# Column sums of the late modulation vectors: from four 32-column products and a second pass to eight products with one moving column

## The chip, the core and the metric

The kernel runs on one NeuronCore of a Trainium2 chip. The metric is device time in microseconds (us) of one execution. The engines are TensorE (PE, its weight loads PEld), VectorE (DVE), ScalarE (ACT), GpSimd (POOL) and SyncE (SP), which issues nearly all DMAs. Each engine takes its instructions in the order in which they stand in its queue.

## What is computed

One layer of a decoder: a gated DeltaNet mixer and a SwiGLU channel mixer, each followed by a residual and a layer norm, with six modulation vectors worked out from a conditioning vector `c`. For one sequence of 256 tokens and a model width of 2048:

```
cond = jax.nn.silu(c)
mod = (cond @ mod_w[i] + mod_b[i])[:, None, :]
sh1, sc1, ga1, sh2, sc2, ga2 = jnp.split(mod, 6, axis=-1)
h = x * (1 + sc1) + sh1
y = gated_deltanet(h, ...)
x = layer_norm(ALPHA_DN * x + (1 + ga1) * y, ln_g[i, 0], ln_b[i, 0])
h = x * (1 + sc2) + sh2
y = swiglu(h, ffn_w_gu[i], ffn_w_down[i])
x = layer_norm(ALPHA_DN * x + (1 + ga2) * y, ln_g[i, 1], ln_b[i, 1])
```

The change touches how `ga1`, `sc2`, `sh2` and `ga2` are worked out. Each has 2048 numbers and is kept as a tile of 128 partitions by 16 columns, so that number 128·j + p stands in partition p of column j.

## The kernel before

**The projections.** All large products are in f32 precision, split in two parts. A weight block of 128 x 1024 is loaded into `raw` (L188), ACT rounds it to `wh` (L197), and DVE subtracts to get the rest `wl` (L198). TensorE then makes three products of 512 columns for each k tile and each of the two token tiles (L233 to L235). A `Group` runs these over its k tiles in chunks of four. The groups go over `w_in`, then `w_out`, then `ffn_w_gu`, then `ffn_w_down`. Between them, the DeltaNet steps (convolution, the solves, the state) run as tasks.

**The late modulation vectors.** `mods_late` works out one vector of 2048 in two halves of 1024 columns. For each half, 16 blocks `mraw` of 128 x 1024 from `mod_w` are loaded by SP (L342, two buffers). DVE multiplies each by one number a partition, from `cond`, and adds it into `macc` (one buffer; L281 for the first, L282 for the other 15). After the sixteenth, `macc` holds 128 partial sums a column, and TensorE has to add them up over the partitions. The half is closed in these steps:
- four products (L361), each with a column of ones, widened to 32 columns, as weights and 256 columns of `macc` as the moving operand; product j goes to the 32 PSUM partitions from 32·j on;
- `to_columns`: ACT copies the 128 x 256 sums from PSUM to SBUF (`sums`, L287), and two products (L290) with 128 columns of `sums` as weights and four columns of the identity as the moving operand turn them into columns, in a second PSUM tile;
- DVE adds `mod_b` and, for three of the vectors, one, and writes eight columns of the vector (L365).

`ga1`, `sc2` and `sh2` are worked out during the `w_in` and `w_out` groups, `ga2` during the `ffn_w_gu` groups: 8 halves. `to_columns` is also called four times at the start, for `sc1` and `sh1`; these calls stay. The PSUM tiles of both steps come from the tag `tp`, of two buffers, which the transposes use too; `sums` shares the tag `hf`, of two buffers.

**What sets the order.** The code gives each piece of work a priority, a due time counted in projection steps (`at`, `spawn`, `advance`). A scheduler deals the instructions out to the engines' queues by these priorities and by its own estimate of when operands are ready. So a change of the instructions in one place can shift others in the queues. The groups over `ffn_w_gu`, but for the first, keep TensorE's instructions in the order in which they are written.

Of the kernel before, what the change touches and what calls it, by code (L numbers as in the profile page):

```python
# [12 lines left out]
OP = mybir.AluOpType  # L13
# [16 lines left out]
def gdn_layer_kernel(ctx: ExitStack, tc: tile.TileContext, x, c, mod_w, mod_b, ln_g, ln_b,  # L30
# [21 lines left out]
    stt = nc.vector.scalar_tensor_tensor  # L52
    mm = nc.tensor.matmul
# [36 lines left out]
    def tp():  # L90
        return psum.tile([128, 512], F32, name="tp", tag="tp", bufs=2)
# [26 lines left out]
    ones = upper[:, 127:128]  # L118
# [14 lines left out]
    p = tp()  # L133
# [16 lines left out]
    p = tp()  # L150
    tr(p[:, :96], brow[:96], ident[:96, :96])
    modb = consts.tile([128, 96], F32, name="modb")
# [126 lines left out]
    def mac(acc, w, k):  # L279
        if k == 0:  # L280
            return ts(acc, w, cond[:, 0:1], None, op0=OP.mult)  # L281
        return stt(acc, w, cond[:, k:k + 1], acc, op0=OP.mult, op1=OP.add)  # L282

    def to_columns(p, hw, nb):

        acc = work.tile([128, 256], F32, name="sums", tag="hf", bufs=2)
        act(acc[:, 0:hw], p[:, 0:hw], AF.Copy)  # L287
        q = tp()
        for i in range(nb):
            mm(q[:, 4 * i:4 * i + 4], acc[:, i * 128:(i + 1) * 128], ident[:, 0:128:32], start=True, stop=True)  # L290
        return q[:, 0:4 * nb].rearrange("p (i j) -> p j i", j=4)
# [44 lines left out]
    def mods_late(dst, j0, plus, every, pin=False):  # L336

        def load(i):
            raw = stream.tile([128, 1024], F32, name="mraw", tag="mraw", bufs=2)
            half, k = divmod(i, KT)  # L340
            c0 = j0 * 128 + half * 1024
            nc.sync.dma_start(raw, mod_w2[k * 128:(k + 1) * 128, c0:c0 + 1024])  # L342
            return raw

        ahead = [load(0)]
        for i in range(2 * KT):
            half, k = divmod(i, KT)
            if i + 1 < 2 * KT:
                ahead.append(load(i + 1))
            if k == 0:  # L350
                acc = work.tile([128, 1024], F32, name="macc", tag="macc", bufs=1)
            yield every / 2
            ins = mac(acc, ahead.pop(0), k)
            if pin and i == 0:
                tc.keep_in_program_order(ins)
            yield every / 2
            if k == KT - 1:
                yield MACW
                p = tp()
                for j in range(4):  # L360
                    mm(p[32 * j:32 * j + 32, 0:256], ones.to_broadcast([128, 32]), acc[:, j * 256:(j + 1) * 256],  # L361
                       start=True, stop=True)
                qv = to_columns(p, 256, 2)
                j = half * 8
                stt(dst[:, j:j + 8].rearrange("p (j i) -> p j i", j=4), qv, plus,  # L365
                    modb[:, j0 + j:j0 + j + 8].rearrange("p (j i) -> p j i", j=4), op0=OP.add, op1=OP.add)


    def h_tiles(tags, names):
# [549 lines left out]
    def late_mods():  # L919
        yield from mods_late(ga1, 32, 1.0, MODEVERY)  # L920
        yield from mods_late(sc2, 64, 1.0, MODEVERY)
        yield from mods_late(sh2, 48, 0.0, MODEVERY)
        tt(A2, lng[:, 0:KT], sc2, op=OP.mult)
        tt(B2, lnb[:, 0:KT], sc2, op=OP.mult)
        tt(B2, B2, sh2, op=OP.add)
# [231 lines left out]
```

## Time and profile before

| | |
|---|---|
| median of 3 runs | 2375.24 us |
| the three runs | 3448.0, 2375.24, 1709.14 us |
| the profiled execution | 1712.19 us, span 1710.4 us |
| granted TensorE clock, mean over the span | 0.994 |
| PE busy | 1656.9 us (97%) |
| DVE busy | 1138.0 us (67%) |
| ACT busy | 875.9 us (51%) |
| HBM | 229 GB/s over the span |

A row of time shows its start and its duration in us; two times in brackets say how long the engine stood idle before it and what ended that. A weight load on PEld runs ahead of the product that uses it, so several rows overlap. The starts of the weight loads show the pace of TensorE more sharply than the products' durations, whose ends are modelled.

### The profile page before, as it was taken

Reading aid. Unit: us, or ns where it says so; the run is one execution under the profiler, and the core shown is the slowest. Engines: PE = TensorE matmul, PEld = TensorE weight load, DVE = VectorE, ACT = ScalarE, POOL = GpSimd, SP = SyncE. Lnnn points to the kernel's source line nnn. Section 1 sums busy time; section 2 is a strip of 40 time slices with the busy share of each in tenths; the row PEclk is TensorE's granted clock in tenths of the full one; section 3 lists DMA queues with packets and bytes.
Section 4 is the critical chain, followed back from the end, with each engine's and each line's share of the span. In section 5 each row is a group of like instructions: output and inputs, shape, how many; then the busy total and the mean of one; then the engine's idle time right before and its main releaser. Section 6 shows DMA issues by size and latency. Waiting matters only on the chain.

```text
span 1710.4 us, 23214 instructions
## 1 busy us (share of the span) xinstructions
PE 1656.9 (97%) x8655; PEld 1322.0 (77%) x8655; DVE 1138.0 (67%) x1641; ACT 875.9 (51%) x1426; POOL 63.1 (4%) x70
## 2 busy tenths in 40 slices
PE   5999999999999999999999999999999999999996
PEld 2666787787887877888787788888888887888885
DVE  2566997958966988948776875765467544555455
ACT  2433679769568667564333644444444443433342
POOL 1000000001001000000000000000000000100002
PEclk9999999999999999999999999999999999999998
DMA  9998795535864777837888586886688666855663
GB/s 345 371 337 288 226 296 184 172 112 161 257 201 122 235 254 231 262 128 266 305 276 283 150 283 192 287 283 192 189 256 285 186 196 209 283 193 190 196 196 112
DMA packets 184434, 392.93 MB, mean 230 GB/s; under 512 B 12176, under 2 KB 14688, under 8 KB 183040
## 3 DMA queue, kind: packets, MB, share of 16 engines
q1 hardware_dynamic: 181952, 378.64, 68.1%
q0 software_dynamic: 2368, 12.80, 2.2%
q8 instruction: 68, 1.11, 0.3%
q14 instruction: 46, 0.38, 0.1%
HBM read 387.18 MB, written 4.21 MB: 229 GB/s over the span
## 4 chain that ended last, share of the span: by engine, by line
PE 73%; DVE 12%; DMA 6%; issue 4%; ACT 3%; POOL 1%; SPq 1%; POOLq 0%; DVEq 0%; ACTq 0%
PE pj L234 20%; PE pj L233 20%; PE pj L235 20%; DMA mraw<-in_mod_w_dram 6%; DVE wl L198 5%; PE gd L234 1%; PE gd L235 1%; DVE macc L282 1%; PE gd L233 1%; ACT wh L197 1%; PE tp L321 1%; DVE X L596 1%; DVE cy L480 1%; DVE tmp L594 1%; DVE LA L571 1%
## 5 line engine op out<-in xcount | busy, mean ns | idle before, releaser
L198 DVE TENSOR_TENSOR wl<-raw,wh 128x1024 fp32r<-128x1024 f32 x518 | 629.8, 1222 | 358.9 <-ACT wh L197 356.0
L197 ACT ACTIVATE wh<-raw 128x1024 fp32r<-128x1024 f32 x518 | 548.0, 1061 | 612.5 <-PE pj L235 443.3
L233 PE MATMUL pj<-wh,h2T 128*128 128x512 f32 x704 | 275.2, 391 | 0.2 <-ACT h2T L983 0.2
L235 PE MATMUL pj<-wh,h2T 128*128 128x512 f32 x704 | 274.5, 390 | 0.4 <-DVE h2T L988 0.4
L234 PE MATMUL pj<-wl,h2T 128*128 128x512 f32 x704 | 274.0, 390 | 0.0
L233 PE MATMUL pj<-wh,hT 128*128 128x512 f32 x640 | 256.5, 403 | 0.0
L234 PE MATMUL pj<-wl,hT 128*128 128x512 f32 x640 | 256.0, 400 | 0.1
L235 PE MATMUL pj<-wh,hT 128*128 128x512 f32 x640 | 255.7, 400 | 0.0
L282 DVE SCALAR_TENSOR_TENSOR macc<-mraw,cond,macc 128x1024 f32<-128x1024 f32 x120 | 153.6, 1280 | 59.1 <-DMA mraw<-in_mod_w_dram 58.5
L235 PEld LDWEIGHTS pj<-wh,h2T 128*128 128x128 f32 x704 | 132.1, 188 | 28.2 <-DVE h2T L988 0.9
L234 PEld LDWEIGHTS pj<-wl,h2T 128*128 128x128 f32 x704 | 132.2, 188 | 27.7 <-DVE wl L198 0.7
L233 PEld LDWEIGHTS pj<-wh,h2T 128*128 128x128 f32 x704 | 132.2, 188 | 27.7 <-ACT h2T L983 0.8
L233 PEld LDWEIGHTS pj<-wh,hT 128*128 128x128 f32 x640 | 120.5, 189 | 26.4 <-issue 3.3
L234 PEld LDWEIGHTS pj<-wl,hT 128*128 128x128 f32 x640 | 120.7, 189 | 24.9 <-DVE wl L198 0.9
L235 PEld LDWEIGHTS pj<-wh,hT 128*128 128x128 f32 x640 | 120.7, 189 | 23.9 <-issue 0.8
L480 DVE SCALAR_TENSOR_TENSOR cy<-tp,cw,cy 128x255 f32<-128x255 f32 (+2 forms) x192 | 85.9, 475 | 1.3 <-ACT cy L476 1.2
L234 PE MATMUL gd<-wl,hT 128*128 128x512 f32 x128 | 51.7, 406 | 1.4 <-DVE wl L198 1.4
L233 PE MATMUL gd<-wh,hT 128*128 128x512 f32 x128 | 49.8, 398 | 1.9 <-DVE part L266 1.0
L235 PE MATMUL gd<-wh,hT 128*128 128x512 f32 x128 | 51.4, 405 | 0.0
L321 PE MATMUL tp<-mraw,cond 128*32 128x256 f32 x368 | 35.4, 470 | 10.9 <-DMA mraw<-in_mod_w_dram 10.9
L234 PE MATMUL pj<-wl,oTc 128*128 128x512 f32 x112 | 43.8, 391 | 0.7 <-DVE wl L198 0.7
L233 PE MATMUL pj<-wh,oTc 128*128 128x512 f32 x112 | 43.9, 392 | 0.0
(399 smaller groups left out, 2253.6 us busy)
## 6 DMA issues: line engine op xcount, KB each, us to landing
raw<-in_gdn_w_in_dram SPq DMA_DIRECT2D x194, 512.0 KB, 4.7
mraw<-in_mod_w_dram SPq DMA_DIRECT2D x192, 512.0 KB, 5.5
raw<-in_ffn_w_gu_dram SPq DMA_DIRECT2D x176, 512.0 KB, 4.4
raw<-in_ffn_w_down_dram SPq DMA_DIRECT2D x88, 512.0 KB, 4.7
raw<-in_gdn_w_out_dram SPq DMA_DIRECT2D x64, 512.0 KB, 5.4
x<-in_x_dram SPq DMA_DIRECT2D x8, 256.0 KB, 6.2
r<-in_x_dram POOLq DMA_DIRECT2D x2, 1024.0 KB, 5.2
x1s<-r POOLq DMA_DIRECT2D x2, 1024.0 KB, 7.0
```

What stands on the lines that cost most here:

```text
L197: act(hi, raw, AF.Copy)
L198: tt(lo, raw, f32(hi), op=OP.subtract)
L233: mm(ps, sh, wh, start=start, stop=False)
L234: mm(ps, sh, wl, start=False, stop=False)
L235: mm(ps, sl, wh, start=False, stop=stop)
L282: return stt(acc, w, cond[:, k:k + 1], acc, op0=OP.mult, op1=OP.add)
L321: mm(p[32 * j:32 * j + 32, 0:hw], cond[:, k:k + 1].to_broadcast([128, 32]), raw[:, kl, j * hw:(j + 1) * hw], start=(k == 0), stop=(k == KT ...
L480: stt(y[:, o + s:o + 256], p[:, o:o + 256 - s], tap(3 - s, ct + i), y[:, o + s:o + 256], op0=OP.mult, op1=OP.add)
L571: stt(la[:, s0 + i], src, sc[:, 0, c, h:h + 1], dm[:, i, None, :].to_broadcast([128, 2, 128]), op0=OP.mult, op1=OP.mult)
L594: tt(tv, LD[:, j + 1:32, j:j + 1].to_broadcast([128, n, m]), X[:, j, None, 0:m].to_broadcast([128, n, m]), op=OP.mult)
L596: tt(X[:, j + 1:32, 0:m], X[:, j + 1:32, 0:m], tv, op=OP.subtract)
```

## The change

The closing of each half is done in one step. The 1024 columns of `macc` are eight blocks of 128 columns; each block is now the weights of a product whose moving operand is the single column of ones. The product's result is one column of 128 sums, which is already the form wanted. Eight products write eight columns of one PSUM tile, and DVE adds `mod_b` from there. The copy on ACT, the second pass and its PSUM tile are not needed in these halves any more.

```
                 yield MACW
+
                 p = tp()
-                for j in range(4):
-                    mm(p[32 * j:32 * j + 32, 0:256], ones.to_broadcast([128, 32]), acc[:, j * 256:(j + 1) * 256],
-                       start=True, stop=True)
-                qv = to_columns(p, 256, 2)
+                for i in range(8):
+                    mm(p[:, i:i + 1], acc[:, i * 128:(i + 1) * 128], ones, start=True, stop=True)
                 j = half * 8
-                stt(dst[:, j:j + 8].rearrange("p (j i) -> p j i", j=4), qv, plus,
-                    modb[:, j0 + j:j0 + j + 8].rearrange("p (j i) -> p j i", j=4), op0=OP.add, op1=OP.add)
+                stt(dst[:, j:j + 8], p[:, 0:8], plus, modb[:, j0 + j:j0 + j + 8], op0=OP.add, op1=OP.add)
```

The file gets two lines shorter, so that lines behind the change have a number lower by two: L365 becomes L364, L676 L674, L805 L803.

The queues of TensorE, at the half that closes in the first group over `w_out` (779 us in the trace; `upper` holds the column of ones, `oTa` and `oTb` are the DeltaNet's output). Before:

```order
L233 MATMUL pj<-wh,oTb 128x512
L234 MATMUL pj<-wl,oTb 128x512
L235 MATMUL pj<-wh,oTb 128x512
L361 MATMUL tp<-macc,upper 32x256 x4
L233 MATMUL pj<-wh,oTb 128x512
L234 MATMUL pj<-wl,oTb 128x512
L235 MATMUL pj<-wh,oTb 128x512
L290 MATMUL tp<-ident,sums 128x4 x2
L233 MATMUL pj<-wh,oTb 128x512
```

And now, at the same place:

```order
L235 MATMUL pj<-wh,oTa 128x512
L233 MATMUL pj<-wh,oTb 128x512
L362 MATMUL tp<-upper,macc 128x1 x8
L234 MATMUL pj<-wl,oTb 128x512
L235 MATMUL pj<-wh,oTb 128x512
L233 MATMUL pj<-wh,oTb 128x512
```

The two visits of TensorE's queue became one, at about the place of the first.

DVE's queue at the half that closes around 634 us (the first of `sc2`; `oq` is the DeltaNet's output and state work, `nat` a projection that ACT has copied), with the engines that a row waits for. Before:

```order
L282 SCALAR_TENSOR_TENSOR macc<-mraw,cond,macc 128x1024 [waits DMAHW1_49,DVE_49]
L805 SCALAR_TENSOR_TENSOR oq_2000<-oq_2000,fo_4480,nat 128x128
L198 TENSOR_TENSOR wl<-raw,wh 128x1024 [waits Activation_49]
L281 TENSOR_SCALAR macc<-mraw,cond 128x1024 [waits DMAHW2_49,DVE_49,PE_49]
L676 SCALAR_TENSOR_TENSOR oq_3831<-gd,negc,oq_3831 128x128 [waits PE_49]
L676 SCALAR_TENSOR_TENSOR oq_3831<-gd,negc,oq_3831 128x128 x3
L198 TENSOR_TENSOR wl<-raw,wh 128x1024 [waits DMAHW3_49,Activation_49]
L365 SCALAR_TENSOR_TENSOR sc_112<-tp,modb 128x8 [waits PE_49]
```

And now:

```order
L282 SCALAR_TENSOR_TENSOR macc<-mraw,cond,macc 128x1024 [waits DMAHW1_49,DVE_49]
L198 TENSOR_TENSOR wl<-raw,wh 128x1024 [waits DMAHW3_49,Activation_49]
L364 SCALAR_TENSOR_TENSOR sc_112<-tp,modb 128x8 [waits PE_49]
L281 TENSOR_SCALAR macc<-mraw,cond 128x1024 [waits DMAHW2_49,DVE_49]
L803 SCALAR_TENSOR_TENSOR oq_2000<-oq_2000,fo_4479,nat 128x128 [waits Activation_49]
L803 SCALAR_TENSOR_TENSOR oq_2000<-oq_2000,fo_4479,nat 128x128 x3
L674 SCALAR_TENSOR_TENSOR oq_3830<-gd,negc,oq_3830 128x128 [waits PE_49]
```

The addition of `mod_b` moved ahead of the next `macc` start and of the state step L674. Up to the first half's closing, at 409 us, the queues are the same but for line numbers; from there to about 960 us neighbouring rows of DVE, ACT and SP change places in many spots.

## Rows read from the trace of the kernel before

**Rows 1.** The page: busy time by engine, the last chain by engine, one group

```profile
PE 1656.9 (97%) x8655; PEld 1322.0 (77%) x8655; DVE 1138.0 (67%) x1641; ACT 875.9 (51%) x1426; POOL 63.1 (4%) x70
...
PE 73%; DVE 12%; DMA 6%; issue 4%; ACT 3%; POOL 1%; SPq 1%; POOLq 0%; DVEq 0%; ACTq 0%
...
L198 DVE TENSOR_TENSOR wl<-raw,wh 128x1024 fp32r<-128x1024 f32 x518 | 629.8, 1222 | 358.9 <-ACT wh L197 356.0
```

**Rows 2.** Windows: stretch, length, busy us PE PEld DVE ACT POOL, clock, DMA, GB/s

```profile
400.00:960.00 560.00, 545.97 (x3169) 439.07 (x3167) 430.68 (x729) 329.31 (x637) 25.09 (x20) 1.00 0.70 230
```

**Rows 3.** Lines L361, L290, L287: count, then shortest/median/longest in ns

```profile
L361 PEld LDWEIGHTS tp<-macc,upper x64: 105/107/109, 409.0 to 1443.3; 128*32 128x32 f32 x64
L290 PEld LDWEIGHTS tp<-ident,sums x48: 186/190/192, 31.0 to 1445.1; 128*128 128x128 f32 x48
L290 PE MATMUL tp<-ident,sums x48: 168/253/273, 31.0 to 1445.1; 128*128 128x4 f32 x48
L287 ACT ACTIVATE sums<-tp x12: 364/384/387, 30.5 to 1444.3; 128x256 f32<-128x256 f32 x12
```

**Rows 4.** Weight loads in order of time, 778.3 to 781.4 us: start, us, instruction, [idle before]

```profile
778.59 0.19 PEld L235 LDWEIGHTS pj<-wh,oTb 128*128 128x128 f32 x1
779.15 0.16 PEld L361 LDWEIGHTS tp<-macc,upper 128*32 128x32 f32 x8 [0.37 <-DVE oTc L828]
779.72 0.19 PEld L233 LDWEIGHTS pj<-wh,oTb 128*128 128x128 f32 x1 [0.41 <-issue]
...
780.06 0.19 PEld L235 LDWEIGHTS pj<-wh,oTb 128*128 128x128 f32 x1
780.29 0.64 PEld L290 LDWEIGHTS tp<-ident,sums 128*128 128x128 f32 x4
780.85 0.19 PEld L233 LDWEIGHTS pj<-wh,oTb 128*128 128x128 f32 x1
...
781.21 0.19 PEld L235 LDWEIGHTS pj<-wh,oTb 128*128 128x128 f32 x1
```

**Rows 5.** Weight loads in order of time, at 415 us and at 1258 us

```profile
415.48 0.52 PEld L290 LDWEIGHTS tp<-ident,sums 128*128 128x128 f32 x4 [0.60 <-ACT sums L287]
...
1257.85 0.19 PEld L235 LDWEIGHTS pj<-wh,h2T 128*128 128x128 f32 x1
1258.39 0.16 PEld L361 LDWEIGHTS tp<-macc,upper 128*32 128x32 f32 x8 [0.35 <-issue]
1259.88 0.52 PEld L290 LDWEIGHTS tp<-ident,sums 128*128 128x128 f32 x4 [1.33 <-ACT sums L287]
1260.32 0.19 PEld L233 LDWEIGHTS pj<-wh,h2T 128*128 128x128 f32 x1
...
1260.67 0.19 PEld L235 LDWEIGHTS pj<-wh,h2T 128*128 128x128 f32 x1
```

**Rows 6.** Weight loads in order of time, 852.7 to 858.4 us (one of four alike)

```profile
852.57 0.19 PEld L234 LDWEIGHTS pj<-wl,oTc 128*128 128x128 f32 x1
852.80 0.19 PEld L235 LDWEIGHTS pj<-wh,oTc 128*128 128x128 f32 x1
853.34 0.14 PEld L361 LDWEIGHTS tp<-macc,upper 128*32 128x32 f32 x2 [0.35 <-issue]
853.89 0.19 PEld L233 LDWEIGHTS pj<-wh,oTc 128*128 128x128 f32 x1 [0.41 <-ACT wh L197]
...
857.15 0.19 PEld L235 LDWEIGHTS pj<-wh,oTc 128*128 128x128 f32 x1
```

**Rows 7.** Weight loads in order of time, L361 at 551 and 634 us

```profile
551.03 0.19 PEld L361 LDWEIGHTS tp<-macc,upper 128*32 128x32 f32 x8 [1.86 <-issue]
...
633.69 0.16 PEld L361 LDWEIGHTS tp<-macc,upper 128*32 128x32 f32 x8 [1.26 <-DVE macc L282]
```

**Rows 8.** Who waited for whom, TensorE, 400 to 960 us: total, times, longest

```profile
PE pj L234 <- DVE wl L198: 4.0, 3, 2.8
```

**Rows 9.** Who waited for whom, SP's queue, whole span: total, times, longest

```profile
SPq L342 <- DVE macc L282: 84.4, 61, 7.1
```

## Prediction

> **What bounds the kernel now.** I read the page first. TensorE is busy for 97% of the span and the chain that ended last runs through it for 73% [rows 1]. The chain's next share is DVE with 12%. ACT, at 51% of the span, hardly appears in it (3%). So work that leaves ACT gives nothing by itself, while time that TensorE gains or loses counts nearly one for one. Next I read one stretch by the table of windows: from 400 to 960 us, in which six of the eight places of this change lie, TensorE is idle for 560 − 546.0 = 14.0 us at a granted clock of 1.00, the 2.4 GHz level [rows 2]. The change can move no more than its own cost, and whatever the new order does to those 14 us.
>
> Then I read the weight loads (PEld) in order of time, because their starts show TensorE's pace. A projection's loads start 0.23 us apart (852.57 and 852.80) [rows 6]. What exceeds that step is the price of something else. I call one closing of a column half a *half*: it sums the 128 partitions of `macc` and turns the sums into columns. There are 8.
>
> **What a half costs now.** A quiet half is the one at 779 us [rows 4]. From the projection load at 778.59 to the one at 780.06 lie three steps, which would be 0.68 us; they take 1.47. So the L361 block of eight 32-column loads costs 0.79 us. Its eight loads of 107 ns are through in 0.16 us [rows 3, 4], so they start within 0.05; the cost is the idle time ahead of it (0.37) and behind it (0.41). Then L290: from 780.06 to 781.21 is 1.15 us for three steps, so its four loads of 128 columns cost 0.47. They have no idle time on either side. A quiet half is 1.26 us, and 8 of them are 10.1 us.
>
> Three kinds of halves cost more:
> - L290 waits for ACT's copy of the sums where too little stands between. At 1258 the stretch from 1257.85 to 1260.67 takes 2.82 us for three steps, that is 2.14 of price, 0.88 more than a quiet half [rows 5]. The last half, at 1443 us, shows the same. At 415 us it is 0.60 us of idle time, where a usual step leaves 0.04 [rows 5], so 0.6 more. Together 2.4 us.
> - At 853 us projections stand between the four matmuls of L361, so the idle pair is paid four times: from 852.80 to 857.15 there are six steps (1.36) in 4.35 us, a price of 2.99 where 0.79 is usual, 2.2 more [rows 6].
> - At 551 and 634 us L361 waits for the last addition into `macc`: 1.86 and 1.26 us idle where a quiet half has 0.37, so 1.5 and 0.9, together 2.4 us [rows 7].
> The sum is 10.1 + 2.4 + 2.2 + 2.4 = 17.1 us.
>
> **What a half costs after.** The new half is eight matmuls whose weights are 128 columns of `macc` and whose moving operand is one column. This is L290's form: weights 128x128 in f32, with four moving columns there. L290 shows 48 loads for 12 calls of two matmuls [rows 3], so an f32 matmul here is two loads, and a half has 16. L290's four loads at 1259.88 are followed by the next projection's at 1260.32, that is 0.11 us each [rows 5]. 16 × 0.11 = 1.76 us, and 8 halves are 14.1 us. No idle pair is due, since L290 has none. ACT's copy and the wait for it are gone, and so are L290 and one PSUM and one SBUF buffer. The interleaved half stays interleaved but pays nothing for it. The wait for `macc` stays: the order puts the block into the same places of TensorE's queue. So 14.1 + 2.4 = 16.5 us, against 17.1: **−0.6 us**.
>
> The bounds of this price: if the two waits for `macc` fall away through the new order, −3.0. At the other end, a load of 128 columns with its matmul could fail to overlap with the next. The nearest row is L290's matmul, 253 ns [rows 3]: 16 × 0.253 = 4.05 a half, 32.4 in all, plus 2.4, against 17.1: +18 us. I take 0.11, because L290 is the same form back to back and shows it.
>
> One rule speaks against the change. The Trainium skill (TensorE: Matmul & The Clock Gate, LDWEIGHTS) prices a weight load by its columns, about columns/1.2 ns. The old half loads 8×32 + 4×128 = 768 columns, the new one 16×128 = 2048; by that page alone the change costs an estimated 1.07 us a half, +8.5 us. The trace agrees with that price for 128 columns (0.11 us), but charges the old half for idle time that the rule does not count.
>
> **ACT and DVE.** The eight ACT copies of 384 ns are 3.1 us [rows 3] on an engine that is idle for half of the span: worth nothing beyond the wait counted above. DVE keeps one small instruction a half. What moves is its place. At 634 us, and likewise at 409, that row stood behind the start of the next `macc`; now it stands ahead of it and waits for TensorE's block. DVE takes its rows in order, so behind it wait the next `macc` addition, the splits that TensorE needs, and on SP's queue the load of the next `mraw`, which waits for the additions already (84.4 us in 61 waits) [rows 9]. Also TensorE reads `macc` for 1.8 us, longer than before, and holds its one buffer so long. This cover is thin only where DVE is the later one: from 400 to 960 us TensorE waited 4.0 us for `wl`, in three waits, the longest 2.8 [rows 8]. I count zero for it in the sum and let it widen the range.
>
> **Rivals.**
> 1. *Only the loads count.* If the idle 0.37 and 0.41 around L361 come not from its 32-column tiles but from something that the new block has too (the switch from the projections' type to plain f32, say), nothing is saved there. Then a half costs 0.79 + 1.76 = 2.55, eight of them 20.4, and the interleaving (2.2) and the waits for `macc` (2.4) remain: 25.0 against 17.1, +8 us: 1720. For it: the new loads are many more. Against it: L290 is plain f32 between projections and has no idle time on either side [rows 4].
> 2. *The new order gains.* From about 410 to 960 us the scheduler deals DVE, ACT and SP differently. If the waits for `macc` vanish (−2.4) and half of TensorE's 14.0 idle us go too (−7), it is −10: 1702. Nothing in the profile says which way the deal falls; behind 960 us little of the order changes.
> 3. *The other side, slower by over 2%.* DVE, held at the new row until TensorE's block is through, hands `wl` out late, and TensorE then waits at the next projection. The price is at most the block's 1.8 us and a late split (1.2 us [rows 1]) in each of the six halves before 960 us, 18 us: 1730. To be slower by 2% (34 us) each of the six would have to lose 5.7 us, twice the longest wait for `wl` that there is now. So it decides only if one late split delays the next groups too. For it: DVE is busy for 431 of these 560 us [rows 2]. Against it: the splits run ahead of TensorE, and SP waits for freed buffers far more than TensorE waits for splits.
>
> **How the numbers follow.** The profiled execution took 1712.2 us (span 1710.4). The median of the runs shown, 2375.2, is not used, since the three lie between 1709.1 and 3448.0 with the lowest beside the profile: 1709 to 1712 is what the kernel takes, and the span accounts for that. 1712.2 − 0.6, and a little less for the lowest run: I say **1711 us**. Chances: about even, between 1706 and 1716, 0.62; rival 1 at about 1720, 0.13; rival 2 at about 1702, 0.14; rival 3 and the unoverlapped loads, +12 to +18, 0.11, with 0.02 of it beyond 34 us. The range leaves out the far end of rivals 2 and 3, 0.15: **1702 to 1724**. A measurement of this kernel tells about 2% (34 us) from no change. To be faster by that, more than twice the idle time of rows 2 would have to vanish: 0.01. Within: 0.97. Slower: 0.02.
>
> **What the new profile would show.** The sums' line should have 128 loads on PEld, 0.11 us apart, with no 0.41 us of idle time behind them, and from projection to projection a half should be 1.8 us longer than the steps. At 1258 and 1443 us the stretch of 2.82 us should become 2.4. ACT should lack eight copies, and TensorE's idle time from 400 to 960 us should be 10 to 16 us. Idle time of 0.4 us around the block proves rival 1. Loads 0.2 us apart or more prove the upper bound. Waits of TensorE for `wl` above 10 us in that stretch prove rival 3. I would be wrong outright if the new order moved the solves or the state steps apart, so that the stretch from 400 to 960 us grew by more than its own eight blocks.

## The result, and the profile after

The changed kernel takes 1729.2 us in the median of 8 executions (1722.5 to 1734.3), the kernel before 1713.6: a ratio of 1.0089, with a 95% interval from 1.0072 to 1.0106. The ratio leaves out two slow executions of the kernel before (2375.2 and 3448.0 us). The change costs about 15 us where I forecast a gain of 0.6. The profiled execution took 1723.5 us.

The page of the changed kernel: busy time by engine, and the chain that ended last, by engine.

```profile
PE 1667.7 (97%) x8687; PEld 1338.0 (78%) x8687; DVE 1138.3 (66%) x1641; ACT 872.5 (51%) x1418; POOL 62.5 (4%) x70
...
PE 76%; DVE 10%; DMA 5%; ACT 4%; issue 4%; POOL 1%; SPq 1%; POOLq 0%; DVEq 0%; ACTq 0%
```

TensorE is busy for 10.8 us longer than in [rows 1], nearly the whole difference between the two spans (11.3); ACT has the eight instructions less. The table of windows of the changed kernel, for the stretch of [rows 2]:

```profile
400.00:960.00 560.00, 549.41 (x3187) 448.19 (x3186) 429.69 (x727) 325.09 (x635) 23.64 (x18) 0.99 0.70 229
```

TensorE idles less here than before (10.6 us in place of 14.0) and is busy for longer, and the granted clock is 0.99 and no longer 1.00. That was the first hint. The block itself is what I had priced. Its line, with the shortest, median and longest duration in ns, and then the weight loads in order of time at the half that answers to [rows 5]:

```profile
L362 PEld LDWEIGHTS tp<-upper,macc x128: 186/192/192, 414.9 to 1456.3; 128*128 128x128 f32 x128
```

```profile
1267.86 0.19 PEld L235 LDWEIGHTS pj<-wh,h2T 128*128 128x128 f32 x1
1268.09 1.98 PEld L362 LDWEIGHTS tp<-upper,macc 128*128 128x128 f32 x16
1269.98 0.19 PEld L233 LDWEIGHTS pj<-wh,h2T 128*128 128x128 f32 x1
1270.09 0.19 PEld L234 LDWEIGHTS pj<-wl,h2T 128*128 128x128 f32 x1
1270.33 0.19 PEld L235 LDWEIGHTS pj<-wh,h2T 128*128 128x128 f32 x1
```

No idle time stands ahead of the block or behind it. From projection to projection there are three steps and 16 loads in 2.47 us, so (2.47 − 0.68) / 16 = 0.112 us a load. Before, the same stretch took 2.82 us [rows 5]: here the change gains 0.35 us, and again at 1454 us.

Behind the second half it looks otherwise. First the weight loads there, then windows of 3 us around them (the seventh number, 1.00 or 0.50, is the granted clock):

```profile
556.87 0.19 PEld L235 LDWEIGHTS pj<-wh,hT 128*128 128x128 f32 x1
558.89 1.86 PEld L362 LDWEIGHTS tp<-upper,macc 128*128 128x128 f32 x16 [1.83 <-issue]
...
561.25 0.19 PEld L233 LDWEIGHTS pj<-wh,hT 128*128 128x128 f32 x1
561.48 0.19 PEld L234 LDWEIGHTS pj<-wl,hT 128*128 128x128 f32 x1
...
562.04 0.33 PEld L233 LDWEIGHTS pj<-wh,hT 128*128 128x128 f32 x1
562.47 0.33 PEld L234 LDWEIGHTS pj<-wl,hT 128*128 128x128 f32 x1
562.89 0.33 PEld L235 LDWEIGHTS pj<-wh,hT 128*128 128x128 f32 x1
```

```profile
556.00:559.00 3.00, 1.56 (x8) 1.01 (x6) 3.00 (x11) 1.21 (x2) 0.00 (x0) 1.00 0.58 167
559.00:561.80 2.80, 2.80 (x21) 2.62 (x22) 2.80 (x9) 1.77 (x2) 0.00 (x0) 1.00 0.75 209
561.80:565.20 3.40, 3.40 (x10) 2.62 (x9) 2.96 (x8) 1.06 (x1) 0.00 (x0) 0.50 0.46 148
565.20:568.60 3.40, 3.40 (x19) 2.83 (x18) 0.78 (x1) 1.86 (x4) 0.00 (x0) 1.00 0.56 154
```

TensorE waits for 1.83 us, runs the block, and then stands at 1.2 GHz for 3.4 us: the projections' loads start 0.43 us apart instead of 0.23. The same comes at 647.1 to 650.5 us, behind the third half's block, where the wait is only 0.35 us. In the kernel before, the wait at this place is as long [rows 7], and the clock stays at 1.00 (its windows, one over the wait, one over the blocks, one behind):

```profile
548.00:551.00 3.00, 1.60 (x8) 0.98 (x6) 3.00 (x11) 1.08 (x3) 0.00 (x0) 1.00 0.56 149
551.00:554.40 3.40, 3.34 (x22) 2.57 (x23) 3.40 (x12) 3.24 (x4) 0.00 (x0) 1.00 0.77 201
554.40:557.80 3.40, 3.40 (x19) 2.82 (x18) 2.92 (x10) 1.93 (x4) 0.00 (x0) 1.00 0.40 134
```

A 3.4 us stretch at half clock costs 1.7 us where TensorE is busy throughout. Between 60 and 1690 us of the span the changed kernel has five (17.1 us in all), the profile of before has one (3.4 us, at 914.4). A second profile of before, taken later, has 10.2 us.

DVE is held, too. What ended its idle time ahead of the new row, from the answer for line L364 (us, times):

```profile
  PE tp L362: 8.8, 6
```

### The profile page after: what moved, and what is told of

It reads as the page before. It is cut to its first block, busy times and chain, and to the rows that moved or that the text cites. A ratio compares the mean times of both kernels' runs of the same rounds, so it can differ in the third digit from the quotient of the medians.

```text
span 1721.7 us, 23272 instructions
## 1 busy us (share of the span) xinstructions
PE 1667.7 (97%) x8687; PEld 1338.0 (78%) x8687; DVE 1138.3 (66%) x1641; ACT 872.5 (51%) x1418; POOL 62.5 (4%) x70
## 4 chain that ended last, share of the span: by engine, by line
PE 76%; DVE 10%; DMA 5%; ACT 4%; issue 4%; POOL 1%; SPq 1%; POOLq 0%; DVEq 0%; ACTq 0%
PE pj L233 21%; PE pj L235 21%; PE pj L234 21%; DMA mraw<-in_mod_w_dram 5%; DVE wl L198 4%; PE gd L234 1%; PE gd L235 1%; ACT wh L197 1%; PE gd L233 1%; DVE macc L282 1%; PE tp L321 1%; DVE cy L478 1%; PE tp L362 1%; DVE X L594 1%; DVE tmp L592 1%
## 5 line engine op out<-in xcount | busy, mean ns | idle before, releaser
L234 PE MATMUL gd<-wl,hT 128*128 128x512 f32 x128 | 51.7, 406 | 1.4 <-DVE wl L198 1.4
```

The costliest lines, as they stand in the source:

```text
L234: mm(ps, sh, wl, start=False, stop=False)
```

## The experiments

Theories: **P**, the block costs more than its loads at 0.112 us. **H**, DVE held at its new row hands everything behind it out late (rival 3). **O**, the loss comes from the other order of the rows around the closing. **C**, the block lets TensorE's clock fall. **A**, formed on the way: what TensorE saves at one place it waits for at the next row that DVE or ACT sets, and what it loses it gets back there. **M**, the block reads `macc` for longer, so the next accumulation starts late.

| kernel | closing, order | us, median | ratio to before, 95% |
|---|---|---|---|
| before_again | old, old | 1712.4 | 0.9992 [0.9979, 1.0004] |
| after_again | new, new | 1727.9 | 1.0088 [1.0071, 1.0104] |
| new_in_old_order | new, old | 1721.6 | 1.0052 [1.0032, 1.0072] |
| old_in_new_order | old, new | 1721.7 | 1.0057 [1.0037, 1.0077] |
| new_in_old_order_add_free | new, old, add free | 1723.4 | 1.0062 [1.0045, 1.0079] |
| add_half_step_later | new, dealt anew | 1721.5 | 1.0049 [1.0030, 1.0068] |
| one_matmul_in_old_order | 1 of 8, old | 1709.8 | 0.9977 [0.9962, 0.9991] |
| sixteen_matmuls_in_old_order | twice, old | 1746.6 | 1.0191 [1.0167, 1.0214] |
| wide64_in_old_order | new, 64 columns, old | 1720.3 | 1.0037 [1.0023, 1.0051] |
| wide64_in_new_order | new, 64 columns, new | 1728.0 | 1.0078 [1.0062, 1.0094] |
| new_shifted | new, two blocks later | 1720.4 | 1.0043 [1.0027, 1.0059] |
| wide64_shifted | 64 columns, two blocks later | 1718.6 | 1.0040 [1.0028, 1.0053] |
| old_shifted | old, two blocks later | 1713.6 | 1.0006 [0.9992, 1.0020] |
| new_order_to_960 | new, new up to 960 us | 1723.4 | 1.0057 [1.0035, 1.0078] |
| new_order_from_960 | new, new behind 960 us | 1721.4 | 1.0043 [1.0026, 1.0059] |
| old_closing_earlier | old, dealt anew | 1720.6 | 1.0042 [1.0023, 1.0061] |
| old_closing_later | old, dealt anew | 1720.4 | 1.0056 [1.0030, 1.0083] |
| new_closing_later | new, dealt anew | 1719.8 | 1.0037 [1.0021, 1.0053] |

Before stood at 1712.1 to 1713.5 us in these series. In a tied kernel the lines are some 100 higher: L331 to L333 are the projections, L296 is `wl`, L459 to L462 the closing, L1138 is `an`.

### Closing and order apart

Each instruction of an engine gets an edge that only sets the order, to the one that stands ahead of it in the other kernel's program. In the traces all rows of TensorE, DVE and ACT outside the closings stand in new_in_old_order in the order of the kernel before, and in old_in_new_order in that of the changed kernel. So closing and order can be exchanged singly.

```diff
+            for i, j in zip(order, order[1:]):
+                tc.add_manual_dep(j, i.name, mybir.DependencyInfo(mybir.DependencyClass.NoSync,
+                                                                  mybir.DependencyReason.DATA), reason="order of before")
...
+        put_in_order(tc, nc)
```

> The new closing (eight matmuls and DVE's add) with every other instruction of TensorE, DVE, ACT, SP and POOL tied to its neighbour in the order in which the kernel before has them; the eight matmuls stand where the first of the old blocks stood, DVE's add where it stood before, and the ACT copies and the second block are gone. Theory O (the loss comes from the other order in which the rows around the closing now stand, not from the closing): the forecast's sum should come true, 1711 to 1715 us beside 1713.6 us of the kernel before, so a ratio of 0.998 to 1.002. Theory H (DVE is held at its add until TensorE's block is through, and what is queued behind it comes late): the add stands later in the queue than in the changed kernel, its 8.8 us of waiting should fall to under 2 us, and the time to 1712 to 1717 us. Theory P (the new block itself costs more than 0.112 us per weight load in the places that matter): the block is the same, so 1726 to 1732 us.

> The reverse: the old closing (four matmuls, ACT copy, two matmuls, DVE's add) with every other instruction of the five engines tied to the order that the changed kernel has; of the closing only the first block is tied, to the place of the new block, and the copy, the second block and the add go where they are ready. Theory O: as slow as the changed kernel, 1724 to 1733 us, ratio 1.006 to 1.011. Theories H and P: the held add and the new block are gone, so 1711 to 1717 us, ratio 0.999 to 1.002.

> The changed kernel once more, its instructions of the five engines tied to its own order (one of the eight blocks then stands together that was spread over a few matmuls): 1727 to 1731 us, ratio 1.007 to 1.011, if the 15 us are the kernel's and not the series'; near 1723 us, ratio 1.0055, if the order's share was mostly the series'.

Both count. The new closing in the old order costs 8 us (1721.6), the new order with the old closing 8 us (1721.7), both together 15. No theory had said that: O wanted 1711 to 1715 for the first, H and P 1711 to 1717 for the second. The 15 us are the kernel's: a second series gives 1727.9.

> The kernel before, unchanged, as a second profile of it: it shows which of the waits that the changed kernels have and the profile of before has not are the execution's and which the kernel's. Two are in question, both in code and order that the closing doesn't touch in new_in_old_order: TensorE waits 1.7 to 2.5 us for DVE's q at 240 us, and 1.7 us for DVE's an at 1281 us, in every changed kernel; the profile of before has neither. If both appear here too, some 3.5 us of each difference between profiles is the execution's; if neither does, they belong to the change. Time 1710 to 1717 us, ratio 0.998 to 1.002.

A second profile of before is needed to read the others. It has the wait for `q` at 240 us (1.5 us, where the first profile has 0.2), so that part of each difference was the execution's. It has 0.3 us of the wait for `an`, where the changed kernel and new_in_old_order have 1.7.

### What the closing costs

```diff
-                for i in range(8):
+                for i in range(1):
...
+                stt(dst[:, j:j + 8], p[:, 0:1].to_broadcast([128, 8]), plus,
```

```diff
-                for i in range(8):
+                for i in 2 * list(range(8)):
```

> new_in_old_order (1721.6 us) with only the first of the eight matmuls in each of the eight halves; seven eighths of the sums are left out, and the add spreads the first column. All orders tied as there. 7 x 2 x 8 = 112 loads of 0.112 us are gone, 12.5 us. Theory P (each load lies on the path and the block's price is all that the new closing adds): 1708 to 1711 us. Theory C with P (the low-clock stretches behind the closings go too, 2 to 4 us): 1704 to 1708 us. Theory A (what TensorE loses at a closing it partly gets back at its next wait for DVE, and what it saves it partly loses there): half of it, 1713 to 1717 us. By the forecast's own reading the kernel before holds 14.7 us of closing, so with 1.8 us of it left it should stand at 1713.5 - 12.9 = 1700.6 us.

> new_in_old_order with the eight matmuls of each half done twice, into the same columns: 128 loads more, 14.3 us. All orders tied. Theory P: 1735 to 1738 us. Theory C with P (a block twice as long with one column moved per load lets the clock fall behind more of the closings, 1.5 us each): 1738 to 1746 us. Theory A: 1727 to 1731 us.

With one matmul instead of eight it is 11.8 us less than new_in_old_order, where the price says 12.5: **the new block's loads cost their price at the end**, P in its plain form. Theory A misses here (1713 to 1717 us). But the forecast's 1700.6 us are missed by 9. Only 1713.4 − 1709.8 + 1.8 = 5.4 us of the old closings count at the end, not the 14.7 that I read at their places (the two long waits ahead of L361 aside). They do vanish at their places: by the starts of the same weight loads in both traces, the steps at the closings add up to −12.6 us. But the span shrinks by 2.0 us only. Elsewhere TensorE's waits grew by 8.8 us (1.8 of it `q`) and shrank by 4.0, two more stretches at half clock took 2.4 net, and the rest lies in the first 60 us and in small steps. Against the second profile of before it is −13.8 us at the closings, +6.3 in the waits, and −6.4 in all. The two largest waits beside `q`, from the weight loads of one_matmul_in_old_order:

```profile
904.44 0.19 PEld L332 LDWEIGHTS pj<-wl,oTa 128*128 128x128 f32 x1 [1.55 <-DVE wl L296]
...
1275.39 0.14 PEld L1146 LDWEIGHTS tp<-ident,an 128*128 128x128 f32 x1
1277.76 0.75 PEld L1146 LDWEIGHTS tp<-ident,an 128*128 128x128 f32 x7 [2.23 <-DVE an L1138]
```

At both TensorE comes earlier than in the profile of before, by 2.8 and 3.9 us, and DVE's row ends only 1.2 and 1.5 us earlier: that is theory A. At 1277 us `an` stands behind additions into `macc` that wait for their transfers. M falls as the sole cause, since here the block holds `macc` for 0.2 us only and the wait for `an` is there all the same. It may have a share: in new_in_old_order DVE waits 2.1 us for the block ahead of the first addition behind this closing, in the kernel before 1.0.

Sixteen matmuls cost 25.0 us more than eight, 14.3 by the price; P (at most 1738) and A (1727 to 1731) miss, and C with P (at most 1746) by 0.6 us. Most of the rest is the clock. Behind each of this kernel's eight blocks comes a stretch at half clock, and ahead of six of them TensorE does not wait. The last one (weight loads, then windows):

```profile
1474.17 3.76 PEld L460 LDWEIGHTS tp<-upper,macc 128*128 128x128 f32 x32
...
1478.71 0.33 PEld L331 LDWEIGHTS pj<-wh,h2T 128*128 128x128 f32 x1
1479.14 0.33 PEld L332 LDWEIGHTS pj<-wl,h2T 128*128 128x128 f32 x1
```

```profile
1474.00:1478.10 4.10, 4.10 (x36) 4.02 (x35) 1.46 (x3) 1.06 (x1) 0.53 (x1) 1.00 0.55 172
1478.10:1481.50 3.40, 3.40 (x9) 2.63 (x9) 0.13 (x1) 0.00 (x0) 0.00 (x0) 0.50 0.88 354
1481.50:1484.90 3.40, 3.40 (x16) 2.79 (x16) 1.23 (x1) 1.06 (x1) 0.00 (x0) 1.00 0.33 125
```

Here 3.6 us of one-column matmuls stand ahead of the fall, with the engine counted as busy throughout; behind the single block at this place (1.8 us, no wait) the clock stays at 1.00. In all this kernel has 44.4 us at half clock between 60 and 1690 us, against 17.1 with eight matmuls: half of the difference, an estimate of what it costs, is 13.7 us, and 14.3 + 13.7 = 28 against 25.0 measured.

### The clock

```diff
-                    mm(p[:, i:i + 1], acc[:, i * 128:(i + 1) * 128], ones, start=True, stop=True)
+                    mm(p[:, 64 * i:64 * i + 64], acc[:, i * 128:(i + 1) * 128],
+                       ones.to_broadcast([128, 64]), start=True, stop=True)
...
+                stt(dst[:, j:j + 8], p[:, 0:512:64], plus, modb[:, j0 + j:j0 + j + 8], op0=OP.add, op1=OP.add)
```

> new_in_old_order with one thing changed: each of the eight matmuls moves 64 columns of ones instead of one, so that the sums stand in 64 like columns, of which the add reads the first. The loads and their spacing of 0.112 us should stay, since the old blocks moved 256 columns in about that time. Theory C (what the new closing costs beyond its loads is the clock: with one column moved per load TensorE counts as little used, and behind the closings at 556, 642 and 960 us some 24 matmuls of 512 columns stand 0.43 us apart instead of 0.23): those stretches vanish, the mean granted clock rises from 0.988 to 0.993 or more, and the time falls by 4 to 6 us to 1715 to 1718 us. Theory M (the block reads the accumulator for 1.8 us instead of 0.4, so the next accumulation, its weights' transfer and what is queued on DVE behind it come late): nothing changes, 1720 to 1723 us. Theory P (the moves don't hide under the loads): slower than 1723 us.

> The changed kernel with 64 columns of ones moved by each of the eight matmuls, and all instructions of the five engines tied to the changed kernel's own order, so that nothing but the columns differs. Theory C: the low-clock stretches behind the closings at 562 and 647 us go, which held 12 matmuls 0.43 us apart, so 3 to 6 us below the changed kernel's 1729 us: 1722 to 1726 us, ratio 1.005 to 1.0075. Theory O (order alone): 1727 to 1731 us. Theory M: 1727 to 1731 us.

First the same places in new_in_old_order: at the second half a window over the wait, one over the block and one behind, then the one behind the third half's block. Then wide64_in_old_order at the second half, its block's loads and two windows, over the end of the wait with the block, and behind:

```profile
551.40:554.40 3.00, 1.54 (x8) 0.97 (x6) 3.00 (x11) 1.14 (x2) 0.00 (x0) 1.00 0.56 152
554.40:556.80 2.40, 2.40 (x19) 2.31 (x20) 2.40 (x7) 1.84 (x2) 0.00 (x0) 0.99 0.74 218
556.80:560.20 3.40, 3.40 (x10) 2.62 (x9) 2.51 (x9) 1.57 (x2) 0.00 (x0) 0.51 0.59 174
...
642.10:645.50 3.40, 3.40 (x10) 2.66 (x9) 3.30 (x10) 0.78 (x2) 0.00 (x0) 0.50 0.85 298
```

```profile
556.36 1.86 PEld L460 LDWEIGHTS tp<-upper,macc 128*128 128x128 f32 x16 [1.86 <-issue]
```

```profile
555.60:558.00 2.40, 1.61 (x15) 1.64 (x15) 2.40 (x8) 1.66 (x2) 0.00 (x0) 1.00 0.85 232
558.00:561.40 3.40, 3.40 (x18) 2.85 (x18) 3.30 (x13) 1.81 (x3) 0.00 (x0) 1.00 0.76 250
```

With 64 columns moved, after the same wait of 1.86 us and in the same 1.86 us of loads, the clock stays at 1.00, behind the third half too. So **the fall behind these two closings is the one-column block's doing**, together with the wait ahead of it. The clocks of all executions agree: their mean is 0.991 in new_in_old_order and 0.990 in the changed kernel, 0.993 and 0.992 with 64 columns, and 0.993 in the kernel before. What it is worth at the end is another matter: the median is 1720.3 us against 1721.6 in the old order (forecast by C: 4 to 6 us less), and 1728.0 against 1727.9 and 1729.2 in the new one, where the profile has other or longer stretches at half clock (at 670.5, 731.9, 929.9 and 974.3 us). The ratios' intervals overlap.

Then the same from the other side: the block moved away from the wait, 8 and 3 rows further down TensorE's queue.

```diff
-L460 MATMUL tp<-upper,macc 128x1 x8
 L331 MATMUL pj<-wh,hT_116 128x512
 L332 MATMUL pj<-wl,hT_116 128x512
...
+L460 MATMUL tp<-upper,macc 128x1 x8
```

> new_in_old_order with the block of the second and third half (551 and 634 us) behind 8 and 3 more rows of TensorE's queue: the 1.46 and 0.5 us that TensorE waits there for DVE's last accumulations are filled with projections and state matmuls, and for DVE nothing comes later. Theory C (wait and one-column block together bring the clock down, 3.4 us at half clock behind each of the two): both stretches vanish, 3.4 us, and the waits too, 2.0 us, so 5.4 us below new_in_old_order's 1721.6 us: 1715 to 1718 us. Theory W (the waits alone are worth something, the clock falls at the block anyway): 1719 to 1721 us. Theory A (what is saved is waited for at the next row that needs DVE): 1720 to 1723 us.

> new_shifted with 64 columns of ones moved by each matmul. Theory C: the clock needs no help any more at these two, so as new_shifted, and 3 to 5 us below wide64_in_old_order (1720.25 us) by the waits alone at most 2: 1716 to 1719 us. If it stays at 1720 us or above, theory A holds for the waits.

> The kernel before with the same two closings moved in the same way (both blocks of matmuls, the second behind 8 more rows so that the copy's cover stays), everything else tied to its own order. There the clock does not fall behind these closings, so theories C and W: 2.0 us of waits gone, 1711 to 1712 us beside 1713.4 us, ratio 0.9985 to 0.9995. Theory A: no change. It is also the candidate for a kernel faster than both.

The windows of new_shifted, where wait and block stood and behind:

```profile
554.40:557.80 3.40, 3.40 (x25) 3.10 (x24) 3.40 (x12) 2.86 (x3) 0.00 (x0) 1.00 0.78 214
557.80:561.20 3.40, 3.40 (x20) 2.65 (x19) 3.40 (x11) 2.14 (x6) 0.00 (x0) 1.00 0.40 141
```

The wait is filled and the clock stays at 1.00, again at 642 us as well, so theory W's fall at the block anyway is out. Locally C is right, yet 1720.4 us lies in theory A's range: of 5.4 us about one shows at the end. wide64_shifted's 1718.6 us lies in C's range (1716 to 1719), 1.7 us below wide64_in_old_order, with intervals that overlap. old_shifted says it most plainly. Two waits of TensorE are filled and no gain is seen (1.0006; the interval allows for 1.4 us at most). It was the candidate for a faster kernel and isn't one.

### DVE held at its row

> As new_in_old_order, but DVE's add is not tied: in three of the eight halves it now stands 3 to 7 rows earlier in DVE's queue than in the kernel before, in one 2 and in one 1 row later. Theory O: the rows around are still those of the kernel before, so 1711 to 1716 us. Theory H: DVE waits at the earlier adds, some 4 to 6 us in all, and the time goes up with a good part of what the changed kernel lost: 1718 to 1724 us. Theory P: 1726 to 1732 us.

```diff
+                yield 0.5
                 j = half * 8
                 stt(dst[:, j:j + 8], p[:, 0:8], plus, modb[:, j0 + j:j0 + j + 8], op0=OP.add, op1=OP.add)
```

> The changed kernel with half a chunk of four depth blocks (about 2.7 us of TensorE's work) between the eight matmuls and DVE's add, so that the add stands 2 to 11 rows later in DVE's queue in seven of the eight halves; nothing is tied, and the rows around are dealt anew. Theory H: the 8.8 us that DVE waits at the adds fall to under 2 us, and the time to 1712 to 1718 us. Theory O: the waits at the add fall too, but the time is that of one more order, anywhere from 1708 to 1735 us, and need not follow the waits. Theory P: 1726 to 1732 us.

With the add tied to its old place DVE never waits at it; left free, it waits as this answer for its line in new_in_old_order_add_free says:

```profile
  PE tp L459: 5.7, 4
```

The time goes from 1721.6 to 1723.4 us, with intervals that overlap; H had asked for 1718 to 1724 where O had 1711 to 1716, and both forms lie 8 to 10 us above before. So in the old order H is worth about 2 us, which the intervals don't tell from nothing. In the new order, where DVE waits 8.8 us at its adds, no run takes the wait away alone. add_half_step_later did not even do what it was for: DVE waits 7.0 us at its adds (8.8 in the changed kernel), and the time falls to 1721.5. That run is one more order.

### The order

The two orders agree between 960 and 1255 us, so they can be cut there.

> The new closing with the changed kernel's order up to about 960 us (all of TensorE's and ACT's differences and most of DVE's and SP's lie there) and the kernel before's order of DVE and SP behind it. Theory O1 (the order's share of the loss, about 7 us between new_in_old_order and the changed kernel, comes from the solves and state steps between 410 and 960 us): as the changed kernel, 1726 to 1731 us. Theory O2 (it comes from DVE's and SP's rows at 1260 to 1300 us, where TensorE waits for DVE's an): as new_in_old_order, 1719 to 1723 us.

> The reverse: the new closing, the kernel before's order up to about 960 us, and the changed kernel's order of DVE and SP behind it (ten short stretches of DVE's rows and five of SP's between 1259 and 1300 us). Theory O1: as new_in_old_order, 1719 to 1723 us. Theory O2: as the changed kernel, 1726 to 1731 us.

By the medians neither part alone carries it: 1723.4 and 1721.4 us, against 1721.6 without and 1728 with both. O1 and O2 each miss one of the two. But the interval of new_order_to_960 (1.0035 to 1.0078) touches that of the whole new order (from 1.0071), so that a larger share of this part isn't excluded. If the two only lose together, that isn't explained.

```diff
-    ALONE, MACW, ZW, OW = 1.5, 1.0, 0.1, 0.3
+    ALONE, MACW, ZW, OW = 1.5, 0.8, 0.1, 0.3
```

> The kernel before with MACW 0.8 instead of 1.0: the old closing's blocks come due a fifth of a chunk (about 1.1 us of TensorE's work) earlier, nothing is tied, and 186 of DVE's 1,199 rows stand elsewhere. Theory O-any (an order dealt anew loses several microseconds whatever the closing): 1718 to 1728 us, ratio 1.003 to 1.008. Theory O-this (only the order that the new closing brings is bad): 1711 to 1716 us, ratio 0.998 to 1.002.

> The kernel before with MACW 1.2: the old closing's blocks come due about 1.1 us later, 136 of DVE's 1,199 rows stand elsewhere. Theory O-any: 1718 to 1728 us, ratio 1.003 to 1.008. Theory O-this: 1709 to 1716 us, ratio 0.997 to 1.002; the waits of 1.5 and 0.8 us at 551 and 634 us may go, but old_shifted gained nothing from that.

> The changed kernel with MACW 1.2, nothing tied. Theory O-any: one more order with the new closing, 1721 to 1735 us, ratio 1.005 to 1.013. Theory O-this: another order than the changed kernel's, so near new_in_old_order, 1718 to 1723 us, ratio 1.003 to 1.006.

(The second and third have 1.2.) With the old closing and its place in the priorities moved by a fifth, either way, the kernel loses 7 to 8 us, as with the new order. For the old closing O-any holds: the order of the kernel before is better than each of those that the scheduler dealt anew, and a change of its closing's form alone deals it anew. With the new closing and 1.2 the time is 1719.8 us, below what O-any had and in the range of O-this: this order and this closing together cost no more than either alone.

Where the new order loses is seen in part, with the old closing. The page of old_in_new_order:

```profile
PE 1657.0 (96%) x8655; PEld 1324.2 (77%) x8655; DVE 1138.7 (66%) x1641; ACT 875.0 (51%) x1426; POOL 62.6 (4%) x70
```

TensorE is busy for as long as before [rows 1] and idle for 61.4 us of the span of 1718.4, against 53.5 and 51.7 in the two profiles of before. (In the changed kernel itself it is idle for 54.0 us and busy for longer, so with the new closing the same order doesn't lose as idle time.) The wait that grew most there, total, times, longest:

```profile
PE tp L1150 <- DVE an L1142: 3.6, 1, 3.6
```

It isn't the reason by itself: old_shifted waits 3.6 us for `an` too and loses nothing, and old_closing_earlier doesn't wait for it and loses 7.5 us.

## Why the prediction was wrong

**The sum was right, and it wasn't the time.** In new_in_old_order, against the profile of before, the steps from load to load at the eight closings add up to −0.4 us (forecast −0.6): +0.1 at 409, +0.8 at 551, +0.3 at 634, +0.5 at 779 and 950, −1.9 at 853, −0.35 at 1258 and 1443. The price of a load (0.112 us), the block without idle time, the interleaved half, the two halves that waited for the copy: all as forecast. Rival 1's number (+8, 1720) is the one measured in the old order, but its mechanism isn't there, since nothing is idle around the block. The loss stands at other rows. Of the 10.2 us between these two profiles half clock takes 5.6 net and TensorE's waits 3.4 (the largest are `an` with 1.9 and `q` with 1.5, most of which before_again has too). Against the second profile of before it is 5.8 us: −1.6 at the closings, 5.5 in the waits, 2.4 at half clock.

**The step that failed first: "time that TensorE gains or loses counts nearly one for one".** I priced at its place what exceeds the projections' step, and took it for the end's. The old halves hold 14.7 us at their places, and 5.4 of the end. The idle 0.37 and 0.41 around L361 and the interleaving's 2.2 us fell away, and TensorE waited for a third to a half of what was saved at rows that DVE or ACT sets. What the new block adds is kept almost whole (11.8 of 12.5 us). The difference, 13.6 − 5.4 = 8.2 us, is 1721.6 − 1713.4 once more, and no second proof. Why the waits take in the old closings' time and not the new block's isn't shown: against one_matmul_in_old_order they are 4.7 and 6.3 us shorter in the two profiles of before, and 0.9 shorter in new_in_old_order, which has 2.5 us more at half clock. The rule of the Trainium skill that I weighed (TensorE: Matmul & The Clock Gate, LDWEIGHTS, columns/1.2 ns) gives an estimated 5.1 us for the old loads and 13.7 for the new. By the old closings' idle time the trace had seemed to speak against it; at the end its numbers lie beside the 5.4 and 13.6 (11.8 + 1.8), and whether by more than chance no run here shows.

**The second: the clock, which I read as 1.00 and left there** [rows 2]. None of the four profiles with the old closing behind the long wait at 551 us has a low stretch behind the second half, nor has the one with a single matmul. Of the six with the block of eight one-column matmuls there, all have it behind the second half and three behind the third, where the length of the wait doesn't decide it (0.35 us with a fall in the changed kernel, 1.22 without one in new_order_to_960). With 64 columns, or with the block moved, it is gone. In the profile of before the only low stretch behind 60 us follows a wait of 2.8 us [rows 8]. At their places the two stretches cost 1.7 us each; at the end the 64 columns bring 1.4 us in the old order and between nothing and 1.2 in the new, which the intervals don't tell from nothing.

**The third: the new order, which I counted at zero.** I had named it (rival 2 as a gain, and "wrong outright" if the stretch from 400 to 960 us grows by more than its blocks). It costs 6 to 8 us, with either closing. Rival 3 is close in time (1730), but its mechanism isn't seen: DVE was held for 8.8 us, yet from 400 to 960 us TensorE did not wait for `wl` of the projections at all (4.0 us before), and tying the add to its old place, which removes the hold, brings about 2 us in the old order. Of what the new profile was to show, TensorE's idle time from 400 to 960 us (10.6, forecast 10 to 16), the eight copies and the 2.47 us came. They were right and told nothing of the end.

**A reading that was wrong and cost nothing:** the wait at 551 us [rows 7] isn't for `macc`, as the prediction and the expectation of new_shifted have it. From the kernel before, the last addition into `macc` of this half, and the row of DVE that ended when the wait did (`cy` is the convolution):

```profile
491.51 1.32 DVE L282 SCALAR_TENSOR_TENSOR macc<-mraw,cond,macc 128x1024 f32<-128x1024 f32 x1
...
550.45 0.47 DVE L480 SCALAR_TENSOR_TENSOR cy<-tp,cw,cy 128x253 f32<-128x253 f32 x1
```

`macc` had been ready for 58 us. By these times the block waits for the PSUM tile `tp` that L480 still reads. The wait stayed with the new closing all the same (1.83 us); the one at 634 us, which is for `macc`, shrank from 1.26 to 0.35.

**Open:** why the old closings' time goes into waits and the new block's doesn't, whether the two parts of the new order lose only together, and which part of the 7 to 8 us of a new deal lies at which row. Profiles of one kernel differ by 4 us, and one profile of each is too few for that.

## What to carry to other kernels

A price read at one place of the busiest engine is not yet what the end gains or loses: 12.6 us of old closings gave 3.6, while 12.5 us of added loads cost 11.8. Follow a change to the next row at which that engine needs another one, and count what is still there behind it; better still, take the piece out and measure. Where a scheduler deals the order, cost the deal by itself: tie all the other instructions to the old order and run the edit alone, before the edit is blamed or praised. And read the granted clock behind a block of matmuls that move one column: here it fell behind a wait with such a block and behind 3.6 us of them, and 64 columns in the same time kept it up.

## What the runs showed of the hardware

- An f32 matmul with 128 columns of weights is two loads here and costs 0.112 us a load, whether 1 column moves or 64: the block of 16 loads is 1.86 us long in both.
- Behind 3.6 us of one-column matmuls without any wait, counted as busy, TensorE was granted 1.2 GHz for 3.4 us, and so it was behind 1.83 us of waiting and one block of 1.86 us. Behind a like wait and a block of the same length with 64 columns it kept 2.4 GHz.
